# Expert places in alternating sizes, with gather, transposes and sums in blocks, in a two-layer diffusion backbone with a routed expert layer

## The chip, the cores and the metric

The kernel runs on one core of a Trainium2 chip. The metric is the device time of one execution in microseconds (us), here the median of three runs.

## The reference

Two layers work on 256 latent tokens behind 256 context tokens, width 1024, all in float32. The first layer is attention beside a convolution, then a dense SwiGLU. The second is a bidirectional state-space mixer, then a layer of eight experts, of which each token uses two. Only the expert layer is touched:

```python
D_MODEL, SEQ, N_EXPERTS, TOP_K, D_FF_EXPERT = 1024, 256, 8, 2, 3584
def swiglu(h, w1, w3, w2):
    return (silu(h @ w1) * (h @ w3)) @ w2
def moe_swiglu(h, w_router, w1, w3, w2):          # h: 256 tokens x 1024
    top_v, top_i = lax.top_k(h @ w_router, TOP_K)
    gates = sum(one_hot(top_i, 8) * softmax(top_v)[..., None], axis=1)
    for e in range(N_EXPERTS):
        out = out + gates[:, e:e+1] * swiglu(h, w1[e], w3[e], w2[e])
    return out
```

The weights of one expert are three matrices of 1024 x 3584 float32, 44.04 MB; eight make 352.3 MB, and each is read once. After this layer come the residual and a last RMS norm.

## The kernel before

All weights are streamed from DRAM. In the expert part a load fills one of 16 SBUF buffers of 1 MB, taken in turn (`ring`, L1637; `net.rings` in `build`), and SyncE's queue (SP) issues every load (L131). A load waits until TensorE (PE) has read what its buffer held before. So DMA can be at most 16 loads ahead of PE.

`run` (L150) goes through a list of units; a unit has views (the loads, called pieces here), a function per 128 weight rows and an end. It places the load of a later piece (`AHEAD` = 14 pieces further) ahead of the current piece's matmuls. The framework then orders each engine's instructions by priority in program order, as operands become ready.

**Places.** There are eight places for experts. Place 0 holds expert 0, whose weights have fixed addresses; places 1 to 7 hold the other experts by falling token count (`places`, L1579), and their loads use a register that SP reads. A place has room for 32 tokens in each of its groups: `G = [3, 3, 3, 3, 2, 2, 2, 2]`. If an expert has more tokens than its place, two conditional passes over all eight experts follow (`moe`, L1643).

**One expert** (`expert`, L1471). `gather` (L1432) compares each token's position with slot numbers (DVE, L1444), and 16 matmuls with that 0/1 matrix collect the tokens, transposed (PE, L1451), which ACT and DVE scale and write to SBUF (L1457, L1459). `up` multiplies by w1 and w3: the hidden width is cut into a part of 2048 (16 pieces of 1 MB: 8 KB per row) and one of 1536 (16 pieces of 768 KB: 6 KB per row). Each group's 32 tokens take 32 columns of the array, and four slices of the width are multiplied side by side, 8 instructions per piece and group in the trace (L1491). SiLU is on ACT (L1499), the product on DVE (L1502). `turn` transposes the hidden values (PE, L1514), and ACT and DVE copy them out (L1519, L1517). `down` multiplies by w2 (L1545), 14 pieces of 1 MB, each two blocks of 128 rows of 4 KB. `scatter` scales the result (DVE, L1555), multiplies with the transposed 0/1 matrix (PE, L1562; the transposes of that matrix are L1466) and adds the gated rows to the stream (DVE, L1566).

**Order.** `experts` (L1627) chains the units: the first `up` of an expert, then the second half of the `down` of the one before and its scatter, then the first transposes, the second `up`, the first half of `down`, the second transposes. Gather, transposes of the 0/1 matrix and scatter are generators that `tick` (L202) advances in the gaps between pieces, so their PE work stands between matmuls of other pieces. `finish` (L1669) does the last norm and stores the output.

Of the kernel before, what the change touches and what calls it, by code (L numbers as in the profile page):

```python
# [19 lines left out]
P = 128  # L20
# [7 lines left out]
NCONST = 1032  # L28


def host_consts():

    kc = np.zeros((P, NCONST), np.float32)
# [12 lines left out]
    ang = np.concatenate([row[:, None] * inv, col[:, None] * inv], axis=-1).astype(f32)  # L46
    cos, sin = np.cos(ang), np.sin(ang)
    cd = np.repeat(cos, 2, axis=1)
    sd = np.stack([-sin, sin], axis=-1).reshape(2 * P, 64)
    kc[:, C_COS:C_COS + P] = cd.reshape(2, P, 64).transpose(1, 0, 2).reshape(P, P)  # L50
    kc[:, C_SIN:C_SIN + P] = sd.reshape(2, P, 64).transpose(1, 0, 2).reshape(P, P)
    for j in range(4):
        kc[32 * j:32 * j + 8, C_SEL8:C_SEL8 + 8] = np.eye(8)
    return kc


class Pair:
# [4 lines left out]
    def __call__(self, k, s=slice(0, 512)):  # L62
        return tuple(t[k // 4][:, k % 4, s] for t in self.t)

# [11 lines left out]
class Net:  # L76
# [44 lines left out]
    def load(self, view, pool=None):  # L121

        pieces = view if isinstance(view, list) else [(slice(0, P), view)]
# [161 lines left out]
    def columns2(self):  # L285
        A, cols, row = self.A, self.cols_fn, self.row_fn
        kc = self.ecp.tile([P, NCONST - C_LE], F32, name="kc")
        self.nc.sync.dma_start(kc, A["kc"][:, C_LE:])
# [1084 lines left out]
    def route(self):  # L1373
# [4 lines left out]
        self.h2 = mp.tile([P, 2, D], F32, name="h2")  # L1378
        m8 = rt.tile([P, 2, 8], F32, name="m8")
# [49 lines left out]
    G = [3, 3, 3, 3, 2, 2, 2, 2]  # L1429
    SS = ((0, 512), (2048, 384))  # L1430

    def gather(self, e, pos, n_g):  # L1432
# [4 lines left out]
        Pm = self.wk([P, 2, 3, 4, 32], "pm", bufs=2)[:, :, :n_g]  # L1437
        x = self.wk([P, KD, 96], "xe", bufs=2)[:, :, :n]
        PT = self.wk([P, 3, 256], "PT", bufs=2)

        def work():
            slots = self.iota[:, :n].rearrange("p (g t) -> p g t", g=n_g).unsqueeze(2).to_broadcast([P, n_g, 4, 32])
            for b in range(2):
                nc.vector.tensor_scalar(Pm[:, b], slots, pos[:, b, e:e + 1], None, op0=ALU.is_equal)  # L1444
            yield
            for q in range(2):
                pt = self.ps("h")
                for i in range(4):
                    k = 4 * q + i
                    for b in range(2):  # L1450
                        nc.tensor.matmul(pt[:, i * n:(i + 1) * n].rearrange("p (g t) -> p g t", g=n_g),  # L1451
                                         self.h2[:, b, k * P:(k + 1) * P], Pm[:, b, :, 0], start=b == 0, stop=b == 1)
# [7 lines left out]
                yield  # L1460

        def turn():
            for g in range(n_g):
                pt = self.ps("h")
                for b in range(2):
                    nc.tensor.transpose(pt[:, b * P:(b + 1) * P], Pm[:, b, g].rearrange("p r t -> p (r t)"), self.ident)  # L1466
                nc.scalar.copy(PT[:, g], pt[:, 0:256])
                yield
        return x, PT, work(), turn()

    def expert(self, e, n_g, nxt=None):  # L1471


        nc, A = self.nc, self.A
        w1, w3, w2 = (self.weights(n, e) for n in ("od_ex_w1", "od_ex_w3", "od_ex_w2"))
        st = {}

        def up(s, i, w):
            c0, n = self.SS[s]

            def begin():
                if s == 0 and i == 0:
                    st["x"], st["PT"], work, st["turn"] = self.xe
                    for _ in work:
                        pass
                st[i] = [self.ps("h") for _ in range(n_g)]
# [17 lines left out]
            return Unit([w[:, k:k + 1, c0:c0 + 4 * n] for k in range(KD)], mm, begin, end, False)  # L1504

        def turn(s):
            nch = self.SS[s][1] // P

            def call():
                st["hT", s] = hT = self.wk([P, 4, 3, P], "hT", bufs=2)  # L1510
                for g in range(n_g):
                    pt = self.ps("h")
                    for c in range(nch):
                        nc.tensor.transpose(pt[:, c * P:(c + 1) * P], st["g"][g][:, c * P:(c + 1) * P], self.ident)  # L1514
                    o, i = hT[:, :nch, g], pt[:, :nch * P].rearrange("p (c t) -> p c t", c=nch)
# [4 lines left out]
                if s == 0:  # L1520
                    self.later(st["turn"], self.R_GA)
                elif nxt is not None:
                    self.xe = nxt()
                    self.later(self.xe[2], self.R_GA)
            return Unit(begin=call)

        def down(s):
            nch = self.SS[s][1] // P
# [5 lines left out]
            def mm(k, wv, _):  # L1534

                p, c = divmod(k, nch)
                st["w", k % 2] = wv, p, c
                if k % 2 == 0:
                    return
                for g in range(n_g):  # L1540
                    for half in range(2):
                        for j in range(2):
                            w, p, c = st["w", j]
                            r = 64 * half + 32 * j
                            nc.tensor.matmul(st["y"][g][r:r + 32], st["hT", s][:, c, g, 32 * p:32 * p + 32],  # L1545
                                             w[:, 512 * half:512 * half + 512], start=s == 0 and k == 1,
                                             stop=s == 1 and k == 4 * nch - 1, tile_position=(0, r))

            k0 = 16 * s
            return Unit([w2[:, k0 + r:k0 + r + 2] for r in range(0, 4 * nch, 2)], mm, begin, None, False)  # L1550

        def scatter():
            ys = self.wk([P, 3, 512], "ys", bufs=2)
            for g in range(n_g):
                nc.vector.tensor_mul(ys[:, g], st["y"][g], self.g2)  # L1555
            yield
            for b in range(2):
                pt = [self.ps("h") for _ in range(2)]
                for g in range(n_g):
                    for half in range(2):  # L1560
                        r = slice(64 * half, 64 * half + 64)
                        nc.tensor.matmul(pt[half], st["PT"][r, g, b * P:(b + 1) * P], ys[r, g], start=g == 0,  # L1562
# [4 lines left out]
                yield  # L1567

        first = [up(0, 0, w1), up(0, 1, w3)]
        second = [turn(0), up(1, 0, w1), up(1, 1, w3), down(0), turn(1)]  # L1570
        return first, second, [down(1), Unit(begin=lambda: self.later(scatter(), 1))]

    def weights(self, name, e):
        w = self.A[name][0]
        if e == 0:
            return w[0].rearrange("(k p) n -> p k n", p=P)
        return w[bass.ds(self.at[e], 1)].rearrange("o (k p) n -> p (o k) n", p=P)

    def places(self):  # L1579
# [15 lines left out]
        nc.vector.tensor_tensor(one, sq(rank, 1), sq(self.iota[:, 0:7], 2), op=ALU.is_equal)  # L1595

        def place(dst, src):
# [6 lines left out]
        ati = mp.tile([P, 7], I32, name="ati")  # L1604
        nc.vector.tensor_copy(ati, at)
        self.at = {e: nc.values_load(ati[0:1, e - 1:e], engines=[mybir.EngineType.SP], min_val=1, max_val=7)
                   for e in range(1, 8)}
# [6 lines left out]
        self.pos, self.gate = pos, gate  # L1614
        cap = mp.tile([P, 8], F32, name="cap")
        for e in range(8):
            nc.gpsimd.memset(cap[:, e:e + 1], 32.0 * self.G[e])
        nc.vector.tensor_copy(over[:, 0:1], cnt[:, 0:1])
        place(over[:, 1:8], cnt[:, 1:8])
        nc.vector.tensor_sub(over, over, cap)  # L1620
# [4 lines left out]
        self.cap = cap  # L1625

    def experts(self, gather, n_g):  # L1627

        units, last = [], []
        for e in range(8):  # L1630
            nxt = (lambda e=e: gather(e + 1)) if e < 7 else None
            a, b, c = self.expert(e, n_g[e], nxt)
            units += a + last + b
            last = c
        return units + last
# [5 lines left out]
    AHEAD = 14  # L1641

    def moe(self):  # L1643
        nc = self.nc
        self.xe = self.gather(0, self.pos, self.G[0])
        for _ in self.xe[2]:
            pass
        self.places()
        units = self.experts(lambda e: self.gather(e, self.pos, self.G[e]), self.G)
        self.run(units, self.AHEAD)  # L1650
        self.fn = self.wk([P, D], "t8")
        nc.sync.dma_start(self.fn, self.A["final_norm"].partition_broadcast(P))
        self.drain()
# [4 lines left out]
        for q in (0, 1):  # L1658
            with self.tc.If(n > 96 * q):
                self.rings = [self.rawp]  # L1660
                p2 = self.wk([P, 2, 8], "p2", bufs=1)
                nc.vector.tensor_tensor(p2, self.pos, self.cap.unsqueeze(1).to_broadcast([P, 2, 8]), op=ALU.subtract)
                nc.vector.tensor_scalar(p2, p2, -96.0 * q, None, op0=ALU.add)
                self.xe = self.gather(0, p2, 3)
                self.run(self.experts(lambda e: self.gather(e, p2, 3), [3] * 8))
                self.drain()
# [89 lines left out]
def build(tc, A, out, dbg=None):  # L1756
# [6 lines left out]
    with ExitStack() as ctx, tc.tile_pool(name="cp", bufs=1) as net.cp, \  # L1763
# [3 lines left out]
        with tc.tile_pool(name="t8p", bufs=9) as net.t8p, ExitStack() as early:  # L1767
# [11 lines left out]
            with psum("psm", h=5, y=3) as net.psp, tc.tile_pool(name="mp", bufs=1) as net.mp:  # L1779
# [3 lines left out]
                with tc.tile_pool(name="ep", bufs=1) as net.wp, tc.tile_pool(name="rawm", bufs=1) as rawm:  # L1783
# [16 lines left out]
```

## Time and profile before

| what | us |
|---|---|
| runs | 1996.44 (median), 1993.87, 1998.35 |
| the profiled execution, its own time | 1998.1 |
| its span, first to last instruction | 1996.3 |
| first expert matmul (L1491) after the span's start | 1088.6 |
| PE busy in the span | 1860.1 (93%) |

The profile is of one execution. Times within it are counted from the start of its span. Engines are PE (TensorE), DVE (VectorE), ACT (ScalarE), POOL (GpSimd) and SP (SyncE's DMA queue). A busy PE is busy by its records, whose ends are modelled.

### The profile page before, as it was taken

Reading aid. Unit: us, or ns where it says so; the run is one execution under the profiler, and the core shown is the slowest. Engines: PE = TensorE matmul, PEld = TensorE weight load, DVE = VectorE, ACT = ScalarE, POOL = GpSimd, SP = SyncE. Lnnn points to the kernel's source line nnn. Section 1 sums busy time; section 2 is a strip of 40 time slices with the busy share of each in tenths; the row PEclk is TensorE's granted clock in tenths of the full one; section 3 lists DMA queues with packets and bytes.
Section 4 is the critical chain, followed back from the end, with each engine's and each line's share of the span. In section 5 each row is a group of like instructions: output and inputs, shape, how many; then the busy total and the mean of one; then the engine's idle time right before and its main releaser. Section 6 shows DMA issues by size and latency. Waiting matters only on the chain.

```text
span 1996.3 us, 29959 instructions
## 1 busy us (share of the span) xinstructions
PE 1860.1 (93%) x12586; PEld 1057.2 (53%) x12586; DVE 734.5 (37%) x1079; ACT 519.0 (26%) x948; POOL 257.7 (13%) x239
## 2 busy tenths in 40 slices
PE   6999999999999989899898999999999999979795
PEld 3685366888888868666566343433434343313121
DVE  3496545333343458988975000101001011101011
ACT  3434443222223247466653000000000000000000
POOL 0154000000000024476650000000000000000000
PEclk8999989999999999999898999999999999999998
DMA  8544575323322332221338999898998999999996
GB/s 295 179 136 155 202 201 179 127 85 106 106 85 95 117 118 85 84 64 64 116 127 313 306 418 364 336 403 289 416 344 342 415 389 416 413 417 413 418 413 236
DMA packets 136429, 488.31 MB, mean 245 GB/s; under 512 B 10432, under 2 KB 15192, under 8 KB 119896
## 3 DMA queue, kind: packets, MB, share of 16 engines
q1 hardware_dynamic: 136280, 486.25, 65.0%
q8 instruction: 103, 1.69, 0.4%
q14 instruction: 46, 0.38, 0.1%
HBM read 485.14 MB, written 1.07 MB: 244 GB/s over the span
## 4 chain that ended last, share of the span: by engine, by line
PE 69%; DMA 14%; DVE 10%; ACT 2%; issue 2%; POOL 1%; SPq 0%; DVEq 0%; ACTq 0%; POOLq 0%
PE h L1491 20%; PE g L226 9%; PE g L227 9%; PE g L228 9%; DMA t<-in_od_ex_w_dram 9%; PE y L1545 8%; DVE cv L1055 5%; DMA raw<-in_od_ex_w_dram 4%; PE h L1562 2%; PE g L330 1%; PE h L1451 1%; PE o L758 1%; PE g L735 1%; DVE whl L147 1%; DMA raw<-in_ev_w_in_dram 1%
## 5 line engine op out<-in xcount | busy, mean ns | idle before, releaser
L1491 PE MATMUL h<-t,xe 128*32 128x384 f32 (+1 forms) x2880 | 288.4, 541 | 13.5 <-DMA t<-in_od_ex_w_dram 13.3
L227 PE MATMUL g<-t,whl 128*128 128x512 f32 (+1 forms) x608 | 237.7, 391 | 0.0
L228 PE MATMUL g<-t,whl 128*128 128x512 f32 (+1 forms) x608 | 236.1, 394 | 0.7 <-POOL whl L147 0.7
L226 PE MATMUL g<-t,whl 128*128 128x512 f32 (+1 forms) x608 | 233.3, 395 | 1.4 <-ACT opad L1033 0.7
L1491 PE MATMUL h<-raw,xe 128*32 128x512 f32 (+1 forms) x2240 | 223.3, 540 | 8.1 <-DMA raw<-in_od_ex_w_dram 8.1
L147 DVE TENSOR_TENSOR whl<-raw,whl 128x1024 fp32r<-128x1024 f32 x109 | 138.6, 1274 | 201.0 <-ACT whl L144 200.6
L144 ACT CAST whl<-raw 128x1024 fp32r<-128x1024 f32 x129 | 134.7, 1050 | 265.6 <-PE g L228 231.2
L1491 PEld LDWEIGHTS h<-t,xe 128*32 128x32 f32 x2880 | 92.0, 110 | 195.3 <-issue 167.9
L1502 DVE TENSOR_TENSOR g<-g,h 128x512 f32<-128x512 f32 (+1 forms) x40 | 24.8, 621 | 458.3 <-PE h L1491 365.4
L411 POOL TENSOR_SCALAR rsv<-sst 128x1 f32<-128x1 f32 (+1 forms) x15 | 5.5, 364 | 1353.6 <-DVE sst L404 1353.5
L227 PE MATMUL g<-whl,t 128*128 128x512 f32 (+1 forms) x432 | 169.3, 394 | 6.4 <-DVE whl L147 3.2
L228 PE MATMUL g<-whl,t 128*128 128x512 f32 (+1 forms) x432 | 166.8, 394 | 0.0
L226 PE MATMUL g<-whl,t 128*128 128x512 f32 (+1 forms) x432 | 162.4, 395 | 2.9 <-DVE t L624 1.4
L1491 PEld LDWEIGHTS h<-raw,xe 128*32 128x32 f32 x2240 | 73.7, 110 | 150.9 <-issue 134.7
L1545 PE MATMUL y<-t,hT 128*32 128x512 f32 x1288 | 144.9, 594 | 8.7 <-DMA t<-in_od_ex_w_dram 8.6
L226 PEld LDWEIGHTS g<-t,whl 128*128 128x128 f32 x608 | 116.0, 192 | 30.1 <-issue 2.3
L228 PEld LDWEIGHTS g<-t,whl 128*128 128x128 f32 x608 | 116.0, 191 | 25.3 <-issue 1.9
L227 PEld LDWEIGHTS g<-t,whl 128*128 128x128 f32 x608 | 116.4, 191 | 23.4 <-issue 0.9
L1519 ACT COPY hT<-h 128x512 f32<-128x512 f32 (+1 forms) x24 | 12.8, 533 | 418.1 <-PE h L1514 417.8
L1545 PE MATMUL y<-raw,hT 128*32 128x512 f32 x952 | 107.9, 594 | 8.8 <-DMA raw<-in_od_ex_w_dram 8.8
L1545 PEld LDWEIGHTS y<-t,hT 128*32 128x32 f32 x1288 | 43.0, 110 | 103.0 <-issue 77.8
L227 PEld LDWEIGHTS g<-whl,t 128*128 128x128 f32 x432 | 82.5, 191 | 27.0 <-DVE whl L147 4.7
(348 smaller groups left out, 2189.3 us busy)
## 6 DMA issues: line engine op xcount, KB each, us to landing
t<-in_od_ex_w_dram SPq DMA_DIRECT2D x135, 1024.0 KB, 12.9
raw<-in_od_ex_w_dram SPq DMA_DIRECT2D x105, 1024.0 KB, 13.9
t<-in_od_ex_w_dram SPq DMA_DIRECT2D x72, 768.0 KB, 9.3
raw<-in_od_ex_w_dram SPq DMA_DIRECT2D x56, 768.0 KB, 10.8
raw<-in_ev_ff_w_dram SPq DMA_DIRECT2D x32, 1024.0 KB, 5.2
raw<-in_ev_ada_w_dram SPq DMA_DIRECT2D x24, 1024.0 KB, 6.9
raw<-in_od_ada_w_dram SPq DMA_DIRECT2D x24, 1024.0 KB, 5.3
raw<-in_od_w_in_dram SPq DMA_DIRECT2D x20, 1024.0 KB, 5.2
```

Source lines behind the costliest of these rows:

```text
L144: self.nc.scalar.copy(hv, v[:, k0:k0 + m])
L147: eng.tensor_tensor(lv, v[:, k0:k0 + m], hv.bitcast(F32), op=ALU.subtract)
L226: mm(out, l[0], r[0], start=start, stop=False)
L227: mm(out, l[0], r[1], start=False, stop=False)
L228: mm(out, l[1], r[0], start=False, stop=stop)
L330: nc.tensor.matmul(st["p"][32 * j:32 * j + 32], self.cs[:, k, 6 - 2 * i:38 - 2 * i], wv, start=k < 4, stop=k >= 4, tile_position=(0, 32 * j))
L735: nc.tensor.matmul(sc[c][:, :nk], self.qT[s, r, b * P:(b + 1) * P], self.kT[s, :nk], start=True, stop=True, tile_position=(64 * c, 0))
L1055: nc.vector.scalar_tensor_tensor(v, pads[i + j][:, 0:ns, t:t + 256], self.cvw(t, c0 + i + j), v, op0=ALU.mult, op1=ALU.add)
L1491: nc.tensor.matmul(st[i][g][32 * p:32 * p + 32, :n], st["x"][:, k, 32 * g:32 * g + 32], wv[:, n * p:n * p + n], start=k == 0, stop=k == KD ...
L1502: nc.vector.tensor_mul(st["g"][g], st["g"][g], st[1][g][:, :n])
L1545: nc.tensor.matmul(st["y"][g][r:r + 32], st["hT", s][:, c, g, 32 * p:32 * p + 32], w[:, 512 * half:512 * half + 512], start=s == 0 and k == 1,
L1562: nc.tensor.matmul(pt[half], st["PT"][r, g, b * P:(b + 1) * P], ys[r, g], start=g == 0, stop=g == n_g - 1, tile_position=(64 * half, 0))
```

## The change

- The groups of the places are now 3, 2, 3, 2, 3, 2, 3, 1. `RANKS` says which rank by token count goes to which place: the largest three of experts 1 to 7 to places 2, 4 and 6, the next three to 1, 3 and 5, the smallest to 7.
- Gather, transposes and scatter are blocks: gather of the next expert stands behind the second `up`, both halves of `down` follow each other, and scatter stands behind the first `up` of the next expert. No generators are left here.
- The transposed 0/1 matrix is no longer made by PE: the positions are written once to DRAM (`pos_rows`, in expert 0, between its w1 and w3), each expert reads its row of 256 positions back to all 128 partitions, and DVE compares it with slot numbers (`slot_map`).
- w2 is loaded as pairs of neighbouring rows, 8 KB, in 12 of the 14 pieces; the hidden values are transposed with a stride of two to match.
- Constants for slots, ranks and capacities are loaded in `route` (`km`). SP reads an expert's register at that expert's first load, no longer all seven in `places`. 17 buffers are in the ring, `AHEAD` is 16.

The diff, cut to its core:

```diff
+GROUPS = (3, 2, 3, 2, 3, 2, 3, 1)
+RANKS = (3, 0, 4, 1, 5, 2, 6)
...
+        km = mp.tile([P, 18], F32, name="km")
+        nc.sync.dma_start(km, self.A["kc"][:, NCONST:])
+        self.slot, self.rank_at, self.cap = km[:, 0:3], km[:, 3:10], km[:, 10:18]
...
-    G = [3, 3, 3, 3, 2, 2, 2, 2]
...
-        Pm = self.wk([P, 2, 3, 4, 32], "pm", bufs=2)[:, :, :n_g]
+        Pm = self.wk([P, 2, 96], "pm", bufs=2)[:, :, :n]
...
+    def slot_map(self, e, n_g):
+        nc = self.nc
+        r = self.wk([P, 256], "prow", bufs=2)
+        nc.sync.dma_start(r.rearrange("p (b t) -> p b t", b=2), self.posd[:, e].partition_broadcast(P))
+        PT = self.wk([P, 3, 256], "PT", bufs=2)
+        for g in range(n_g):
+            nc.vector.tensor_scalar(PT[:, g], r, self.slot[:, g:g + 1], None, op0=ALU.is_equal)
+        return PT
+
+    def pos_rows(self, pos):
...
+        nc.tensor.transpose(pt[:16, 0:P], pos.rearrange("p b e -> p (b e)"), self.ident)
+        r = self.wk([16, P], "posr", bufs=1)
+        nc.scalar.copy(r, pt[:16, 0:P])
+        d = self.drp.tile([16, P], F32, name=self.nm("posd"))
+        nc.sync.dma_start(d, r)
...
         def turn(s):
...
-                    for c in range(nch):
-                        nc.tensor.transpose(pt[:, c * P:(c + 1) * P], st["g"][g][:, c * P:(c + 1) * P], self.ident)
+                    for c in range(n // P):
+                        t = st["g"][g][:, c // 2 * 256:c // 2 * 256 + min(256, n - c // 2 * 256)]
+                        if t.shape[-1] == 256:
+                            t = t.rearrange("p (i j) -> p j i", j=2)[:, c % 2]
+                        nc.tensor.transpose(pt[:, c * P:(c + 1) * P], t, self.ident)
...
         def down(s):
+            pair = lambda w: w.rearrange("o (i j) n -> i (o j) n", j=2)
...
+        def evict():
+            st["PT"] = self.slot_map(e, n_g)
+            st["ys"] = ys = self.wk([P, 3, 512], "ys", bufs=1)
             for g in range(n_g):
                 nc.vector.tensor_mul(ys[:, g], st["y"][g], self.g2)
...
+        return ([Unit(begin=take), up(0, 0, "od_ex_w1"), up(0, 1, "od_ex_w3")],
+                [turn(0), up(1, 0, "od_ex_w1"), up(1, 1, "od_ex_w3")], [turn(1), down(0), down(1)],
+                Unit(begin=scatter))
...
         for e in range(8):
...
+            a, b, c, d = self.expert(e, n_g[e])
+            units += a + scatter + b + gather(e + 1) + c
+            if e == 0 and now:
+                units.insert(2, Unit(begin=now))
+            scatter = [d]
...
-    AHEAD = 14
+    AHEAD = 16
...
-                    net.rings = ["t8"] * 9 + [net.rawp] * 3 + [net.hlp] * 3 + [rawm]
+                    net.rings = ["t8"] * 9 + [net.rawp] * 3 + [net.hlp] * 3 + [rawm] * 2
```

## Rows read from the trace of the kernel before

**Rows 1.** The page, part 2: GB/s moved, in 40 slices of the span.

```profile
GB/s 295 179 136 155 202 201 179 127 85 106 106 85 95 117 118 85 84 64 64 116 127 313 306 418 364 336 403 289 416 344 342 415 389 416 413 417 413 418 413 236
```

**Rows 2.** Busy time by stretch: PE, PEld, DVE, ACT, POOL; clock, DMA share, GB/s.

```profile
1049.00:1088.00 39.00, 31.36 (x164) 25.98 (x163) 23.21 (x73) 14.20 (x25) 2.10 (x12) 0.87 0.93 357
1150.00:1200.00 50.00, 50.00 (x513) 21.78 (x509) 3.73 (x8) 2.69 (x6) 0.00 (x0) 1.00 1.02 418
1437.00:1560.00 123.00, 123.00 (x1185) 46.66 (x1186) 11.74 (x21) 8.19 (x17) 0.00 (x0) 1.00 0.94 357
1088.00:1655.00 567.00, 567.00 (x5448) 217.98 (x5451) 55.20 (x99) 40.05 (x82) 0.00 (x0) 1.00 0.95 363
1655.00:1748.00 93.00, 88.26 (x802) 29.70 (x795) 10.62 (x20) 6.17 (x14) 0.00 (x0) 1.00 1.02 414
1748.00:1855.00 107.00, 91.92 (x802) 28.78 (x802) 9.32 (x16) 5.61 (x12) 0.00 (x0) 1.00 1.02 415
```

**Rows 3.** The chain that ended last, from 1088 us: start, us, what.

```profile
1088.66 41.34 PE h L1491 x384
1130.00 1.53 PE h L1514 x12
...
1190.07 41.34 PE h L1491 x384
...
1313.53 41.34 PE h L1491 x384
...
1560.42 27.61 PE h L1491 x256
```

**Rows 4.** Timeline of SP's queue, 960 to 1092 us: start, us, what.

```profile
1077.13 0.33 SPq L131 DMA_DIRECT2D raw<-in_od_ex_w_dram  x1
1091.44 0.33 SPq L131 DMA_DIRECT2D t<-in_od_ex_w_dram  x1
```

**Rows 5.** Groups by line, 1190 to 1313 us: busy us, mean ns, idle before.

```profile
L1491 PE MATMUL h<-t,xe 128*32 128x512 f32 (+1 forms) x432 | 42.4, 540 | 0.0
L1491 PE MATMUL h<-raw,xe 128*32 128x512 f32 (+1 forms) x336 | 33.0, 540 | 0.0
L1545 PE MATMUL y<-t,hT 128*32 128x512 f32 x168 | 18.4, 592 | 0.0
L1545 PE MATMUL y<-raw,hT 128*32 128x512 f32 x168 | 18.4, 592 | 0.0
L1562 PE MATMUL h<-ys,PT 64*128 64x512 f32 x24 | 6.7, 606 | 0.0
...
L1466 PE MATMUL h<-ka,pm 128*128 128x128 f32 x6 | 1.3, 300 | 0.0
```

**Rows 6.** Timeline of PE where DMA sets the pace: pieces of 6, 8, 4 KB rows.

```profile
1723.10 1.50 PE L1491 MATMUL h<-t,xe 128*32 128x384 f32 x16 [0.38 <-DMA t<-in_od_ex_w_dram]
1725.00 1.50 PE L1491 MATMUL h<-t,xe 128*32 128x384 f32 x16 [0.41 <-DMA t<-in_od_ex_w_dram]
...
1748.01 1.92 PE L1491 MATMUL h<-raw,xe 128*32 128x512 f32 x16 [0.65 <-DMA raw<-in_od_ex_w_dram]
...
1785.24 1.92 PE L1491 MATMUL h<-raw,xe 128*32 128x512 f32 x16 [0.59 <-DMA raw<-in_od_ex_w_dram]
...
1792.90 1.92 PE L1545 MATMUL y<-t,hT 128*32 128x512 f32 x16 [0.64 <-DMA t<-in_od_ex_w_dram]
...
1800.55 1.92 PE L1545 MATMUL y<-t,hT 128*32 128x512 f32 x16 [0.61 <-DMA t<-in_od_ex_w_dram]
...
1855.30 1.92 PE L1491 MATMUL h<-raw,xe 128*32 128x512 f32 x16 [0.65 <-DMA raw<-in_od_ex_w_dram]
```

**Rows 7.** DMA issues: count, KB each, median us from issue to landing.

```profile
t<-in_od_ex_w_dram SPq DMA_DIRECT2D x135, 1024.0 KB, 12.9
...
dtpar<-in_od_dt_bias_f_dram SPq DMA_DIRECT2D x1, 16.0 KB, 2.8
```

**Rows 8.** Timeline of all engines behind the last landing.

```profile
1973.98 1.92 PE L1545 MATMUL y<-raw,hT 128*32 128x512 f32 x16 [0.62 <-DMA raw<-in_od_ex_w_dram]
...
1975.12 0.69 DVE L1555 TENSOR_TENSOR ys<-y,g2r 128x512 f32<-128x512 f32 x1 [33.54 <-PE y L1545]
1975.86 3.70 PE L1562 MATMUL h<-ys,PT 64*128 64x512 f32 x16
```

More of the change, by code (lines that the diff above doesn't have):

```diff
@@ L1502, in end, with take @@
                         nc.vector.tensor_mul(st["g"][g], st["g"][g], st[1][g][:, :n])
-            return Unit([w[:, k:k + 1, c0:c0 + 4 * n] for k in range(KD)], mm, begin, end, False)
+            view = lambda k: self.weights(name, e, [P, 1, 4 * n], lambda w: w[:, k * P:(k + 1) * P, c0:c0 + 4 * n]
+                                          .rearrange("o p n -> p o n"))
+            return Unit([view(k) for k in range(KD)], mm, begin, end, False)
+        def take():
+            st["x"] = self.xe
         def turn(s):
-            nch = self.SS[s][1] // P
+            n = self.SS[s][1]
             def call():
@@ L1519, in call @@
                         nc.scalar.copy(o, i)
[L1520 to L1524, printed above, removed]
             return Unit(begin=call)
         def down(s):
-            nch = self.SS[s][1] // P
+            r0, n = 4 * self.SS[s][0] // 4, self.SS[s][1]
+            rows = lambda r, m: (lambda w: w[:, r:r + m])
+            pair = lambda w: w.rearrange("o (i j) n -> i (o j) n", j=2)
+            pieces = []
+            for p in range(4):
+                for c in range(n // 256):
+                    f = rows(r0 + n * p + 256 * c, 256)
+                    pieces.append((lambda w, f=f: pair(f(w)), [(p, 2 * c), (p, 2 * c + 1)]))
+            if n % 256:
+                for p in (0, 2):
+                    f = rows(r0 + n * p, 2 * n)
+                    pieces.append((lambda w, f=f: f(w).rearrange("o (s i) n -> i (o s) n", s=2)[n - P:n],
+                                   [(p, n // P - 1), (p + 1, n // P - 1)]))
             def begin():
@@ L1542, in mm, with scatter @@
                         for j in range(2):
-                            w, p, c = st["w", j]
+                            p, c = at[j]
                             r = 64 * half + 32 * j
                             nc.tensor.matmul(st["y"][g][r:r + 32], st["hT", s][:, c, g, 32 * p:32 * p + 32],
[L1546 to L1553, printed above, removed]
+                                             st["w", j][:, 512 * half:512 * half + 512], start=s == 0 and k == 1,
+                                             stop=s == 1 and k == 4 * n // P - 1, tile_position=(0, r))
+            return Unit([self.weights("od_ex_w2", e, [P, 2, D], f) for f, _ in pieces], mm, begin,
+                        evict if s else None, False)
+        def evict():
+            st["PT"] = self.slot_map(e, n_g)
+            st["ys"] = ys = self.wk([P, 3, 512], "ys", bufs=1)
             for g in range(n_g):
                 nc.vector.tensor_mul(ys[:, g], st["y"][g], self.g2)
-            yield
+        def scatter():
             for b in range(2):
@@ L1566, in scatter, with weights, get @@
                     nc.vector.scalar_tensor_tensor(x, pt[half], self.gate[:, b, e:e + 1], x, op0=ALU.mult, op1=ALU.add)
[L1567 to L1577, printed above, removed]
+        return ([Unit(begin=take), up(0, 0, "od_ex_w1"), up(0, 1, "od_ex_w3")],
+                [turn(0), up(1, 0, "od_ex_w1"), up(1, 1, "od_ex_w3")], [turn(1), down(0), down(1)],
+                Unit(begin=scatter))
+    def weights(self, name, e, shape, f):
+        def get():
+            if e and e not in self.at:
+                self.at[e] = self.nc.values_load(self.ati[0:1, e - 1:e], engines=[mybir.EngineType.SP], min_val=1,
+                                                 max_val=7)
+            return f(self.A[name][0][bass.ds(self.at[e], 1) if e else slice(0, 1)])
+        return View(shape, get)
     def places(self):
@@ L1613, in places @@
                 place(dst[:, b, 1:8], src[:, b, 1:8])
[L1614 to L1617, printed above, removed]
+        self.gate = gate
+        self.pos2 = pos
         nc.vector.tensor_copy(over[:, 0:1], cnt[:, 0:1])
         place(over[:, 1:8], cnt[:, 1:8])
-        nc.vector.tensor_sub(over, over, cap)
+        nc.vector.tensor_sub(over, over, self.cap)
         mx = small("mxc", 1)
@@ L1624, in places, with experts, gather, call @@
         nc.vector.tensor_copy(self.cnt, mx)
-        self.cap = cap
-    def experts(self, gather, n_g):
-        units, last = [], []
-        for e in range(8):
[L1631 to L1635, printed above, removed]
+    def experts(self, n_g, now=None):
+        units, scatter = [], []
+        def gather(e):
+            def call():
+                self.xe, work = self.gather(e, n_g[e])
+                work()
+            return [Unit(begin=call)] if e < 8 else []
+        for e in range(8):
+            a, b, c, d = self.expert(e, n_g[e])
[3 more added lines that the diff above has]
+            scatter = [d]
+        return units + scatter
     def ring(self):
```

89 lines of the change are left out of this document (42 added, 47 removed).

## The prediction

> **What bounds the kernel now.** I read the throughput line first [rows 1]: from slice 22 on, at about 1090 us, the experts' weights stream. Up to slice 33 the rate swings between 289 and 418 GB/s, and from there to the end it stands at 413 to 418, but for single slices. The table by stretch says why [rows 2]. From 1088 to 1655 us PE is busy all the time (567 of 567 us), at a granted clock of 1.00, and DMA moves 363 GB/s. From 1655 to 1855 PE is busy 180 of 200 us and DMA moves 414 to 415. So two limits follow each other: PE for the places with three groups, DMA for those with two. The reader should see that each limit leaves the other resource idle in its half.
>
> The chain [rows 3] gives the sizes. The first product starts at 1088.66; a place with three groups takes 1313.53 - 1190.07 = 123.5 us; the fifth expert, the first with two groups, starts at 1560.42. In the DMA half the same step comes at 1748.01 and 1855.30 [rows 6], 107.3 us apart, and there PE waits 0.4 to 0.65 us for DMA before each piece. SP's queue [rows 4] shows how DMA is held back: after the load at 1077.13 all 16 buffers are taken (I count three expert loads before 1049 us and 13 from there), and the next goes out at 1091.44, when PE has read the first piece.
>
> **The change, part by part.**
>
> *Order of the places.* 567 us at 363 instead of 414 GB/s are 567 x (1 - 363/414) = 69.8 us of streaming lost to a full ring [rows 2]. Alternating places remove this if PE, over a pair, needs less than DMA. PE: of a three-group expert, 42.4 + 33.0 + 18.4 + 18.4 + 6.7 + 1.3 = 120.2 us are products that go by the number of groups [rows 5]; the third of them is 40.1. The transposes of the 0/1 matrix (1.3 for three groups) go. That leaves 122.2 us for three groups, 123.5 - 40.1 - 0.9 = 82.5 for two, some 43 for one. That a third is right shows in the first product, 41.34 against 27.61 [rows 3]. DMA: pieces land 37.23/15 = 2.48 us apart for 8 KB rows, 1.90 for 6 KB rows, 7.65/3 = 2.55 for w2's 4 KB rows [rows 6]. Before that is 16 x 2.48 + 16 x 1.90 + 14 x 2.55 = 105.8 us for an expert, 1.5 less than the 107.3 seen, which I add. After, with 12 of w2's pieces at 2.48, 106.5 us. A pair is 204.7 us on PE and 213 on DMA: DMA sets the pace, and 4 us per expert are free on PE. Three-group places let DMA gain 15 us on PE, two-group places take back 24; the ring holds some 40 us, so it neither fills nor matters after the first expert.
>
> *What stays lost.* Expert 0 begins with a full ring. From 1088 to 1091.4 nothing goes out: 3.4 us. Its first product reads 16 buffers in 41.3 us, refilled by 16 loads of 1.90: 10.9 us. The rest of expert 0, 80.9 us, frees 30 buffers, refilled in 30 x 2.49 = 74.7: 6.2. Together 20.5 us. The 17th buffer takes one more load ahead of 1088: -2.5.
>
> *w2 in 8 KB rows.* 8 x 12 x 0.07 = -6.6 us. Bounds: nothing if the rows go out as 4 KB after all, to 8 us if the other two pieces gain as well.
>
> *Slot map by comparison.* PE's transposes are counted above. Added are eight reads of 128 KB in 512 B rows. No row has such a read in a full stream. From below 128 KB at 414 GB/s, 0.3 us; from above the 2.8 us in which 16 KB land alone [rows 7], most of that latency. The step from 8 to 4 KB rows costs 0.07 us for 128 packets more, so 256 packets cost some 0.14: I take 0.5 us, +4 together, and keep 2 to 22. The DVE comparisons take the place of larger ones, on an engine that is idle nine tenths of the time [rows 2]. By the Trainium skill (DMA: Bandwidth & Descriptors, "Measured") a transfer of 64 KB takes 0.95 us; an estimate from that, 1.9 us for each read, would make the sum 11 us longer; no run here shows it.
>
> *Waits that are added.* The read stands on SP behind the next expert's first 16 loads. DVE waits for it; behind it on DVE stand the scaling of the result and the next expert's gate products, and PE waits for both in scatter. But those 16 loads are what PE works on until scatter, and the read lands right behind the last, so I take 0 to 3 us, within the 4 that are free. The one store of the positions lets SP wait until PE has transposed them, between w1 and w3 of expert 0; loads behind it wait for buffers of that same moment: 0 to 2 us. The constants' load stands beside the load of g2's row, which already waits for its memory: 0, at worst a few us of a stream that idles from about 1084 anyway. SP's register reads move to each expert's first load, where up to 16 loads are under way: 0.
>
> *Gather, transposes, sums in blocks.* The same PE instructions in another order. What hid DVE's gate product before the second transposes was half of `down`; now it is the gather. Where nothing covers it, in expert 0, the transposes start right at the end of the product and take 1.53 us [rows 3]. So 0 to 2 us for each expert, within the 4 free; if that cover is gone, each us costs 7 to 8 us.
>
> *Tail.* Before, the last piece lands at 1973.98 and the span ends 22.3 us later. With one group instead of two, half of the 3.70 us of sums and one scaling of 0.69 go [rows 8], and the last comparison, some 1 us, comes: -1.5.
>
> Sum: -69.8 + 20.5 - 2.5 - 6.6 + 4 - 1.5 = -55.9. Against the profiled execution's own time, 1998.1, that is 1942.2; this execution was 1.7 us over the median shown (1996.44), so a median of 1940.5.
>
> **The rivals.**
>
> *PE becomes the bound.* If waits of the blocks come to more than 4 us per expert, the pairs go by PE. At 8 us the excess is 4 x 7 = 28 us: 1968.5. For it: scatter uses four PSUM tiles at once and stands between products that need three, of five; the strided transposes may be slower. Against: the covers above, and 1.53 us without any.
>
> *The stream gives no more beside a busy PE.* In the first half DMA moves 357 to 363 GB/s because its rate is capped while PE never pauses, not because buffers are late. Then alternating brings nothing, and -6.6 + 4 - 1.5 are left: 1992.3. Against it stands one row: from 1150 to 1200 us PE is busy 50.00 of 50 us, and DMA moves 418 GB/s [rows 2]. The Trainium skill (DMA: Bandwidth & Descriptors, "Where 436 GB/s comes from") has a rule of this kind: from HBM a core gets some 358 GB/s, which binds. By that rule the first half is at the limit and the change is worth nothing there; the trace disagrees, with 414 GB/s and more from 1655 to 1855 us.
>
> *Slower: the position read comes late.* If SP sends the read only when the product that it should run beside is done, it lands behind a queue of loads, and scatter, and PE with it, waits each time. A load's median from issue to landing is 12.9 us [rows 7], a full queue is 16 x 2.5 = 40. The point from which this decides is (55.9/7) + 4 = 12 us per expert; at 20 us it is 7 x 16 = 112 us: 2052. For it: SP issues in order, and DVE stands still behind the read. Against: the read depends on nothing that is late, the 40 us of the next product stand between it and its use.
>
> *The places don't hold the tokens.* Then a second pass of eight experts would follow, over 850 us. On the reference's drawn inputs the router gives the experts 81, 90, 60, 39, 16, 83, 91 and 52 tokens. Ranked, 91, 90 and 83 fit 96, then 60, 52 and 39 fit 64, 16 fits 32, and expert 0's 81 fit 96. So its chance is 0.
>
> **How the numbers follow.** The forecast: 0.76. PE the bound, with a gain left: 0.14. The capped stream: 0.02. The late read: 0.06, half of it strong enough to come out slower than before, plus 0.02 for other mishaps of order. Late reads that still leave a gain are faster too; the capped stream and part of the borderline make "same". A measurement of this kernel tells about 0.2% from no change. So faster 0.91, same 0.03, slower 0.06. The range: down to 1928, where the full rate of 418 GB/s instead of 414 holds (8 us less) and expert 0 loses 4 us less; up to 1964, where the reads cost near their upper bound or the blocks expose 7 us per expert. That leaves out the rest of the PE case, the late read and the cap, somewhat under 2 in 10.
>
> **What would show it.** Right: from expert 1 on the rate stands at 412 or more in every stretch, PE waits for DMA at the end of each two-group expert, starts of a pair are some 213 us apart, the last landing is at about 1919, the place with one group has PE less than half busy, w2's pieces land 2.48 us apart. Wrong: PE busy throughout with the rate below 400 after expert 1 (the blocks), idle time of PE ahead of the sums (L1562 before) that ends with DVE or the position read (late read), a rate near 360 with free buffers (the cap), or a second pass.

## The result, and the profile after

The changed kernel takes 1943.2 us (median of four runs, 1940.9 to 1944.9), the kernel before in the same comparison 1995.2. The ratio is 0.9737, with a 95% interval of 0.9719 to 0.9755: 52.5 us less, against 55.9 in the forecast. The profiled execution took 1942.3 us, its span is 1940.4 us.

Busy time by stretch of the changed kernel, about one expert to a stretch (two are left out), then the end (columns as in [rows 2]; from 1391 us on PE begins an expert up to 19 us behind the start of its stretch):

```profile
1085.00:1201.00 116.00, 116.00 (x1162) 46.47 (x1165) 11.90 (x37) 9.11 (x18) 0.00 (x0) 1.00 0.92 357
1201.00:1285.00 84.00, 84.00 (x810) 33.28 (x806) 10.23 (x22) 4.93 (x10) 0.00 (x0) 1.00 1.02 417
1285.00:1391.00 106.00, 106.00 (x1061) 42.65 (x1057) 11.06 (x22) 6.80 (x14) 0.00 (x0) 1.00 1.02 418
1391.00:1494.00 103.00, 101.08 (x938) 35.65 (x934) 12.70 (x24) 4.96 (x10) 0.00 (x0) 1.00 1.02 418
...
1604.00:1706.00 102.00, 97.63 (x898) 33.72 (x890) 11.79 (x21) 4.96 (x10) 0.00 (x0) 1.00 1.01 418
...
1811.00:1916.00 105.00, 80.29 (x575) 17.70 (x571) 6.14 (x9) 2.15 (x4) 0.00 (x0) 0.83 0.96 396
1916.00:1941.00 25.00, 5.04 (x16) 1.18 (x8) 7.93 (x13) 2.89 (x8) 1.48 (x4) 0.57 0.14 49
```

Where [rows 2] had 363 GB/s over 567 us, the stream now stands at 417 to 418 from the second expert on, until it runs out in the last stretch, and it does so beside a PE that is busy 106 of 106 us. Only expert 0 is left at 357. There 116 x (1 - 357/418) = 16.9 us of streaming are lost, where 69.8 were lost before.

The chain that ended last (answering to [rows 3]) alternates with the places:

```profile
1085.71 20.74 PE h L1515 x192
...
1201.18 27.47 PE h L1515 x256
...
1285.54 41.20 PE h L1515 x384
...
1345.75 18.05 DMA raw<-in_od_ex_w_dram
...
1706.54 23.38 PE h L1515 x216
```

The first product (L1515, L1491 before) starts at 1085.71. A two-group expert that does not wait takes 1285.54 - 1201.18 = 84.4 us (82.5 in the forecast). From 1345 us on DMA stands in the chain, which it did not before 1668 us in the old kernel. The whole stage, first product to last landing, is 1915.3 - 1085.7 = 829.6 us; before it was 1974.0 - 1088.7 = 885.3.

SP's queue of the changed kernel (answering to [rows 4]) shows the full ring and the reads that the change adds:

```profile
1074.28 0.81 SPq L148 DMA_DIRECT2D raw<-in_od_ex_w_dram  x2
1088.91 17.93 SPq L148 DMA_DIRECT2D t<-in_od_ex_w_dram  x8
1107.27 0.33 SPq L1498 DMA_DIRECT2D posd<-posr  x1
1111.12 1.43 SPq L1483 DMA_DIRECT2D prow<-posd  x2
...
1549.41 0.38 SPq L1483 DMA_DIRECT2D prow<-posd  x1
```

The last load of the full ring goes out at about 1075, the next at 1088.91. The position reads are not behind the loads that I put them behind: four of the eight go out by 1117 us, and the last at 1549, hundreds of us ahead of its use. The framework moves a read forward as soon as a buffer for it is free.

PE's timeline where DMA sets the pace (answering to [rows 6]; L1586 is the product with w2), and the last piece:

```profile
1696.50 1.92 PE L1586 MATMUL y<-t,hT 128*32 128x512 f32 x16 [0.57 <-DMA t<-in_od_ex_w_dram]
1698.99 1.92 PE L1586 MATMUL y<-t,hT 128*32 128x512 f32 x16 [0.56 <-DMA t<-in_od_ex_w_dram]
1701.52 1.92 PE L1586 MATMUL y<-t,hT 128*32 128x512 f32 x16 [0.61 <-DMA t<-in_od_ex_w_dram]
1704.05 1.92 PE L1586 MATMUL y<-t,hT 128*32 128x512 f32 x16 [0.61 <-DMA t<-in_od_ex_w_dram]
...
1915.33 1.93 PE L1586 MATMUL y<-raw,hT 128*32 128x512 f32 x8 [0.58 <-DMA raw<-in_od_ex_w_dram]
```

w2's pieces now land 2.49 us apart, the last two of an expert, which kept 4 KB rows, 2.53. The last piece lands at 1915.33 and the span ends 25.1 us later, where it was 22.3 before. Eight instructions take as long there (1.93 us) as sixteen did in [rows 8]: the granted clock is 0.83 in the last stretch of the stream and 0.57 in the end, with one group of work for each piece. These are means of times at PE's two levels, 1.2 and 2.4 GHz.

### The profile page after: what moved, and what is told of

It reads as the page before. It is cut to its first block, busy times and chain, and to the rows that moved or that the text cites. A ratio compares the mean times of both kernels' runs of the same rounds, so it can differ in the third digit from the quotient of the medians.

```text
span 1940.4 us, 29063 instructions
## 1 busy us (share of the span) xinstructions
PE 1810.1 (93%) x12164; PEld 1046.5 (54%) x12164; DVE 732.0 (38%) x1093; ACT 509.5 (26%) x927; POOL 257.3 (13%) x231
## 4 chain that ended last, share of the span: by engine, by line
PE 65%; DMA 17%; DVE 11%; ACT 3%; issue 2%; POOL 1%; SPq 0%; ACTq 0%; DVEq 0%; POOLq 0%
PE h L1515 19%; PE g L243 9%; PE g L244 9%; PE g L245 9%; DMA raw<-in_od_ex_w_dram 8%; DMA t<-in_od_ex_w_dram 8%; PE y L1586 6%; DVE cv L1072 6%; PE h L1605 1%; PE g L347 1%; PE h L1468 1%; PE o L775 1%; PE g L752 1%; DVE whl L164 1%; DMA raw<-in_ev_w_in_dram 1%
## 5 line engine op out<-in xcount | busy, mean ns | idle before, releaser
L1515 PE MATMUL h<-t,xe 128*32 128x512 f32 (+1 forms) x2576 | 254.4, 544 | 6.5 <-DMA t<-in_od_ex_w_dram 6.5
L1515 PE MATMUL h<-raw,xe 128*32 128x384 f32 (+1 forms) x2288 | 226.7, 542 | 8.3 <-DMA raw<-in_od_ex_w_dram 8.3
L1515 PEld LDWEIGHTS h<-t,xe 128*32 128x32 f32 x2576 | 89.8, 110 | 160.4 <-issue 122.4
L1515 PEld LDWEIGHTS h<-raw,xe 128*32 128x32 f32 x2288 | 80.8, 110 | 141.2 <-issue 104.7
L1586 PE MATMUL y<-t,hT 128*32 128x512 f32 x1168 | 135.8, 616 | 10.7 <-DMA t<-in_od_ex_w_dram 10.7
L1523 ACT ACTIVATE g<-h 128x512 f32<-128x512 f32 (+1 forms) x38 | 20.7, 544 | 442.9 <-PE h L1515 442.9
L245 PEld LDWEIGHTS g<-t,whl 128*128 128x128 f32 x608 | 115.9, 191 | 25.1 <-issue 1.9
L1586 PE MATMUL y<-raw,hT 128*32 128x512 f32 x960 | 111.1, 613 | 5.0 <-DMA raw<-in_od_ex_w_dram 5.0
L1597 DVE TENSOR_TENSOR ys<-y,g2r 128x512 f32<-128x512 f32 x19 | 13.1, 692 | 248.3 <-PE y L1586 248.3
```

The costliest lines, as they stand in the source:

```text
L245: mm(out, l[1], r[0], start=False, stop=stop)
L1515: nc.tensor.matmul(st[i][g][32 * p:32 * p + 32, :n], st["x"][:, k, 32 * g:32 * g + 32], wv[:, n * p:n * p + n], start=k == 0, stop=k == KD ...
L1523: nc.scalar.activation(st["g"][g], st[0][g][:, :n], AF.Silu)
```

## The experiments

Differences below are those of the ratios to the kernel before in the same comparison, against 0.9737 for the changed kernel, times 1995 us. The interval of a ratio is some 0.002 to either side, so such a difference is good to about 5 us. Where it helps, the length of the stage in the profiled execution is given too, first product to last landing (829.6 us in the changed kernel, 885.3 before): it leaves out the start and the end of the kernel.

**The order alone, taken away.**

```diff
-GROUPS = (3, 2, 3, 2, 3, 2, 3, 1)
-RANKS = (3, 0, 4, 1, 5, 2, 6)
+GROUPS = (3, 3, 3, 3, 2, 2, 2, 2)
+RANKS = (0, 1, 2, 3, 4, 5, 6)
```

> The changed kernel with the old order and sizes of the places (3, 3, 3, 3, 2, 2, 2, 2 groups, by falling count); all else as changed. Theory (the order keeps DMA streaming): while the four large places run, PE sets the pace and the ring is full, so most of the 70 us of lost streaming come back; carried load by load I get 45 us over the changed kernel, 1988 us (1980 to 1996), rate about 360 to 370 GB/s over the first four experts. Rival (the other parts made the gain: one group fewer, 8 KB rows, the 17th buffer, blocks): at most 10 us over the changed kernel, 1953 or less.

Measured: 1986.2 us, ratio 0.9939 (0.9918 to 0.9960), 40 us over the changed kernel; the stage is 874.8 us, 45 longer. Busy time by stretch, the four large places and the rest:

```profile
1090.00:1570.00 480.00, 480.00 (x4697) 188.06 (x4693) 47.86 (x101) 29.72 (x60) 0.00 (x0) 1.00 0.93 362
1570.00:1960.00 390.00, 348.68 (x3136) 114.76 (x3132) 37.88 (x68) 17.73 (x36) 0.00 (x0) 1.00 1.01 417
```

(This kernel has one group more, in a place where PE waits for DMA.) The two limits are back, one behind the other: 362 GB/s beside a PE without a pause, then 417 beside one that waits.

**The order alone, put into the kernel before.**

```diff
-    G = [3, 3, 3, 3, 2, 2, 2, 2]
+    G = [3, 2, 3, 2, 3, 2, 3, 1]
+    RANKS = [3, 0, 4, 1, 5, 2, 6]
...
-        nc.vector.tensor_tensor(one, sq(rank, 1), sq(self.iota[:, 0:7], 2), op=ALU.is_equal)
+        rank_at = mp.tile([P, 7], F32, name="rankat")
+        for i, r in enumerate(self.RANKS):
+            nc.gpsimd.memset(rank_at[:, i:i + 1], float(r))
+        nc.vector.tensor_tensor(one, sq(rank, 1), sq(rank_at, 2), op=ALU.is_equal)
```

> The kernel before with nothing changed but the sizes and order of its places (3, 2, 3, 2, 3, 2, 3, 1) and the ranks that go with them; generators, PE-made 0/1 transposes, 4 KB rows of w2, 16 buffers stay. Theory: nearly all the gain, less 8 KB rows (7 us) and one buffer (2.5 us), plus no position reads (4 us): 46 to 52 us below before, 1943 to 1950 us, rate 410 to 416 GB/s from the second expert on. Rival (the other parts made the gain): within 15 us of before.

Measured: 1949.4 us against 1997.6, ratio 0.9769 (0.9746 to 0.9792): 46 us less than before; the stage is 837.7 us, 48 shorter. Its stretches, expert 0 and most of the rest:

```profile
1088.00:1204.00 116.00, 116.00 (x1163) 43.89 (x1159) 7.49 (x14) 9.42 (x20) 0.00 (x0) 1.00 0.96 359
1204.00:1900.00 696.00, 679.12 (x6276) 246.64 (x6268) 72.38 (x124) 42.77 (x90) 0.00 (x0) 0.99 1.02 413
```

From both sides, the order is worth 40 to 46 of the 52 us, and 45 to 48 of the 55.7 by which the stage became shorter. All the rest of the rewrite is worth some 6 to 12.

**w2's rows.**

```diff
-                        t = st["g"][g][:, c // 2 * 256:c // 2 * 256 + min(256, n - c // 2 * 256)]
-                        if t.shape[-1] == 256:
-                            t = t.rearrange("p (i j) -> p j i", j=2)[:, c % 2]
+                        t = st["g"][g][:, c * P:(c + 1) * P]
...
-            pair = lambda w: w.rearrange("o (i j) n -> i (o j) n", j=2)
+            pair = lambda w: w.rearrange("o (j i) n -> i (o j) n", j=2)
```

> The changed kernel with w2 in two blocks of 128 rows of 4 KB for each piece, and transposes without a stride. Theory: 96 pieces land 0.07 us later each, 6.6 us over the changed kernel, w2's pieces 2.55 us apart where DMA sets the pace. Rival (row size costs nothing in a full stream, the 418 GB/s have another cause): no change within 2 us. Third: the strided transposes cost PE more than the rows give, then it is faster than the changed kernel.

Measured: 1951.5 us (1942.9 to 1956.4), ratio 0.9763 (0.9736 to 0.9790), 5 us over the changed kernel; the intervals overlap, so the time alone does not settle it. The trace does: its stage is 837.1 us, 7.5 longer, where 6.6 were foreseen. First two pieces of w2 in a row, then one stretch of this kernel:

```profile
1704.95 1.92 PE L1584 MATMUL y<-t,hT 128*32 128x512 f32 x16 [0.62 <-DMA t<-in_od_ex_w_dram]
1707.52 1.92 PE L1584 MATMUL y<-t,hT 128*32 128x512 f32 x16 [0.64 <-DMA t<-in_od_ex_w_dram]
```

```profile
1201.00:1900.00 699.00, 669.48 (x6284) 242.94 (x6276) 73.16 (x136) 37.46 (x76) 0.00 (x0) 0.98 1.02 414
```

and the same stretch of the changed kernel:

```profile
1201.00:1900.00 699.00, 673.61 (x6284) 247.87 (x6276) 71.92 (x135) 37.41 (x76) 0.00 (x0) 0.98 1.01 417
```

The pieces are 2.57 us apart instead of 2.49, and the rate falls to the 414 that the kernel before had. Its 414 GB/s were no limit of the stream: they were the mean over rows of 8, 6 and 4 KB.

**The small place second.** `GROUPS = (3, 1, 3, 2, 3, 2, 3, 2)`, `RANKS = (6, 0, 3, 1, 4, 2, 5)`.

> The changed kernel with the place of one group second instead of last: 3, 1, 3, 2, 3, 2, 3, 2. Theory (DMA sets the pace, where the small place stands does not matter): the last landing stays within 3 us; only the end changes, as PE keeps its higher clock with two groups: the time from last landing to the end falls from 25.1 to about 22.5 us; total 0 to 4 us below the changed kernel. Rival (the ring's lead is needed from place to place, and a small place early wastes it): 10 us or more over the changed kernel.

Measured: 1941.8 us, ratio 0.9719 (0.9702 to 0.9736), 4 us less by ratio, 1.4 by medians, not resolved. The last landing is at 1915.70, 0.4 us from that of the changed kernel: where the small place stands does not matter to the stream. The end took 24.6 us, not the 22.5 of the theory. Over the fourteen traces of this study the end lies between 21.4 and 25.1 us, and it falls into two parts at the last DVE instruction of the norm (L1728). Up to the end of that instruction two groups take 13.0 us, here and in the kernel before. One group takes 11.5 to 13.3 us, in the same order in which the eight instructions of the last product take 1.06 to 1.94 us. Here is first the changed kernel (13.3 us; its last product is shown above), then the run in which PE makes the 0/1 matrix (11.6 us; told below), from the last product on:

```profile
1918.07 3.78 PE L1605 MATMUL h<-ys,PT 64*128 64x512 f32 x8 [0.81 <-DVE ys L1597]
...
1927.88 0.75 DVE L1728 TENSOR_SCALAR t<-t,rs 128x1024 f32<-128x1024 f32 x1 [0.95 <-POOL rs L430]
```

```profile
1911.21 1.07 PE L1585 MATMUL y<-raw,hT 128*32 128x512 f32 x8 [1.47 <-DMA raw<-in_od_ex_w_dram]
1913.18 1.99 PE L1604 MATMUL h<-ys,PT 64*128 64x512 f32 x8 [0.91 <-DVE ys L1596]
...
1922.02 0.75 DVE L1727 TENSOR_SCALAR t<-t,rs 128x1024 f32<-128x1024 f32 x1 [0.95 <-POOL rs L430]
```

So one group saves 1.5 us of the end at the higher clock, and PE's lower level (1.2 GHz) takes that back. The second part, in which the last store of the output goes out, takes between 9.3 us (the kernel before) and 12.3 (the run with 4 KB rows), and what sets it stays open.

**The price of a position read, two tries.**

```diff
+        for _ in range(4):
+            r2 = self.wk([P, 256], "prow2", bufs=4)
+            nc.sync.dma_start(r2.rearrange("p (b t) -> p b t", b=2), self.posd[:, e].partition_broadcast(P))
```

> The changed kernel with each expert's read of its positions issued four more times, into buffers that nobody reads: 32 reads more, 128 KB in 512 B rows each. Theory (0.5 us of stream each, as I took): 16 us over the changed kernel (10 to 22). Rival 1 (the estimate from the page, 1.9 us each): 61 us. Rival 2 (a read costs the 2.8 us of the small load alone): 90 us. If the reads cost only their bytes, 0.3 us, 10 us.

Measured: 1973.7 us, ratio 0.9893, 31 us over the changed kernel, 0.97 us for each read, between the theory and Rival 1. But all 32 went out between 1113 and 1198 us, before expert 0 had ended, and they held up the other loads: SP sent nine loads of weights between 1113 and 1153 us, some 19 in the changed kernel. So the try was made again, each set of reads held back by a small DVE instruction that reads it:

```diff
+        self.more = [self.wk([P, 256], "prow2", bufs=4) for _ in range(4)]
+        for r2 in self.more:
+            nc.sync.dma_start(r2.rearrange("p (b t) -> p b t", b=2), self.posd[:, e].partition_broadcast(P))
...
+            for r2 in self.more:
+                j = self.wk([P, 1], "junk", bufs=2)
+                nc.vector.tensor_tensor(j, r2[:, 0:1], ys[:, 0, 0:1], op=ALU.mult)
```

> Again four more reads of the positions for each expert, but each set is read by a small DVE instruction behind the expert's scaling, so that the next set cannot go out earlier than that: the reads are spread over the stage. If a read costs 0.95 us of stream: 27 to 33 us over the changed kernel. If 0.5 us: 13 to 19. If the 30 us of the first try came from their crowding in expert 0 (SP's queue, landing order) and not from a price for each: under 10 us.

Measured: 1972.0 us, ratio 0.9887 (0.9872 to 0.9902), 30 us over the changed kernel, 0.94 us for each read (by the stage 29.2 us, 0.91). The stretch that stands at 417 GB/s in the changed kernel is now at 406, and shows the price spread over the stage:

```profile
1201.00:1900.00 699.00, 663.68 (x6177) 242.47 (x6169) 73.47 (x160) 36.88 (x75) 0.00 (x0) 0.99 1.00 406
```

128 KB at 418 GB/s would take 0.31 us, so two thirds of the price are not the bytes. Two things may make them: the 256 rows of 512 B, or that all 128 partitions read the same 1 KB of DRAM. No run here separates the two.

**More PE work in each expert.** The gather's matmuls done twice, and five times:

```diff
-                    for b in range(2):
+                    for b in list(range(2)) * 2:
```

> The changed kernel with the gather's matmuls of every expert done twice: some 3.7 us more on PE for each expert. Theory (DMA sets the pace, 3 to 4 us per expert are free on PE): 3 to 7 us over the changed kernel, 3.7 of which are expert 0's own gather ahead of the stage. Rival (PE is the bound after all): 8 x 3.7 = 30 us over it.

Measured: 1949.3 us, ratio 0.9763 (0.9744 to 0.9782), 5 us over the changed kernel, where 30 would be PE's. The stage is 1.7 us longer; the rest lies ahead of it, where expert 0's own gather stands.

> The same with the gather done five times: some 15 us more on PE for each expert. Theory: 15 us ahead of the stage for expert 0's own (some of it while the ring is full anyway), then PE becomes the bound, each expert after the first costs 15 less the 4 that are free: 6 to 7 x 11 = 66 to 77, together 80 to 92 us over the changed kernel. Rival (much more PE time is free than I counted): under 50 us. Rival (PE is the bound already): 8 x 15 = 120 us.

Measured: 2037.8 us, ratio 1.0215 (1.0189 to 1.0242), 95 us over the changed kernel, a little above the 80 to 92 of the theory; 80 of them lie in the stage. The chain of this kernel:

```profile
1229.01 27.47 PE h L1515 x256
...
1284.75 18.04 PE h L1468 x160
1327.66 41.20 PE h L1515 x384
...
1460.65 27.47 PE h L1515 x256
```

A pair takes 1460.65 - 1229.01 = 231.6 us here, all PE's, and DMA can do one in 2 x 44.04 MB / 418 GB/s = 211. The gather took 3.7 and takes 18.0: 14.3 us more in each expert, 28.6 in a pair, of which 231.6 - 211 = 21 come out as time. So 8 us of a pair were free, 4 in each expert, as counted. The two runs bracket the point at which PE takes over.

**The floor of the stream.** One group in every place.

```diff
-GROUPS = (3, 2, 3, 2, 3, 2, 3, 1)
+GROUPS = (1,) * 8
...
-    kc[:, C_CAP:C_CAP + 8] = 32 * np.array(GROUPS)
+    kc[:, C_CAP:C_CAP + 8] = 256
```

> The changed kernel with one group in every place: at most 32 tokens for each expert are computed, the others are left out, and no second pass follows. All weights are still streamed. Theory (the stream is the floor, and only expert 0 holds it back): the 17 us of streaming lost in expert 0 go and nothing else, 1922 to 1930 us, rate 418 GB/s throughout. Rival (a busy PE slows the stream a little): the rate goes above 421 GB/s and the time falls below 1918 us.

Measured: 1923.5 us, ratio 0.9642 (0.9619 to 0.9665), 19 us below the changed kernel.

```profile
1085.00:1130.00 45.00, 37.48 (x328) 12.97 (x328) 4.28 (x16) 5.85 (x12) 0.00 (x0) 0.93 0.94 377
1130.00:1900.00 770.00, 534.82 (x2961) 119.42 (x2959) 44.58 (x90) 24.19 (x52) 0.00 (x0) 0.71 1.01 415
```

With less than half of the PE work, the second stretch streams at 415 GB/s as a whole, its running out included, and at 418 to 419 from 1200 to 1800 us, hardly faster than beside a busy PE. All that PE still costs the changed kernel is some 19 us, 17.2 of them in the stage, about the 16.9 lost in expert 0.

**PE makes the transposed 0/1 matrix again, and the buffers of the ring.**

```diff
-        nc.sync.dma_start(r.rearrange("p (b t) -> p b t", b=2), self.posd[:, e].partition_broadcast(P))
...
+            for b in range(2):
+                nc.tensor.transpose(pt[:, b * P:(b + 1) * P], Pm[:, b, g].rearrange("p r t -> p (r t)"), self.ident)
+            nc.scalar.copy(PT[:, g], pt[:, 0:256])
```

> The changed kernel with the transposed 0/1 matrix made by PE again (as a block behind the last half of down), without the store of the positions, the eight reads and the wide comparisons. Theory (a read costs the stream what the four-fold reads showed, 30 us / 32 = 0.95 us, PE has 3 to 4 us free per expert and this takes 1.3 at most): 4 to 8 us below the changed kernel. Rival (0.5 us for each read, as I predicted): 2 to 4 us below. Rival (the PE-made matrix stands in PE's way at each expert's end): 5 us or more above.

Measured: 1935.1 us, ratio 0.9705 (0.9691 to 0.9718), 6 us (8 by medians) below the changed kernel. The two profiled spans are 7.0 us apart. Of these, 1.0 lies ahead of the first product, 2.9 in the end, with the difference in clock that is told above, and 3.2 in the stage. Only the last can be put down to the reads. It is 0.4 us for each of the eight, 0.6 if the 1.3 us of transposes in expert 0 [rows 5], where PE sets the pace, stand against it in full: by these two traces less than an added read costs. Half of the eight go out in expert 0, where the stream is held up anyway; that this is the reason is not shown. The one part of the change that takes work from PE and gives it to DMA was a loss, of some 3 us.

> The same, with the place of one group second instead of last and an 18th buffer in the ring (the transposed matrix has one buffer for it). Theory: the stream starts one load further ahead, -2.5 us, the end is 1 to 3 us shorter: 7 to 13 us below the changed kernel, 1930 to 1936 us, the fastest. Rival (buffers are not what holds the stream in expert 0): no better than the run with PE's matrix alone.

Measured: 1935.4 us, ratio 0.9706: no better than with PE's matrix alone, against my theory. Its last piece lands at 1908.77, 2.4 us ahead of that run's 1911.21, as 18 buffers promised, but its end took 24.1 us against 22.2: with two groups it takes 13.1 us up to the norm's last instruction, with one, at the higher clock, 11.6.

> The changed kernel with 16 buffers in the ring instead of 17. Theory (only expert 0 meets a full ring, one load less ahead): 2.5 us over the changed kernel, 1 to 4. Rival (17 buffers are needed from place to place): 8 us or more. Rival (the number of loads under way is limited elsewhere): 0.

Measured: 1941.7 us, ratio 0.9738 (0.9724 to 0.9751): no difference. Again the last landing (1917.24) is 1.9 us later than with 17 buffers and the end (22.6 us) 2.5 shorter. The stretches of this kernel, then of the changed one:

```profile
1085.00:1127.00 42.00, 42.00 (x386) 14.13 (x389) 4.92 (x24) 4.07 (x7) 0.00 (x0) 0.99 0.73 245
1127.00:1165.00 38.00, 38.00 (x445) 21.55 (x437) 5.12 (x12) 4.26 (x9) 0.00 (x0) 1.00 1.01 412
```

```profile
1085.00:1127.00 42.00, 42.00 (x389) 13.95 (x388) 4.93 (x23) 4.07 (x7) 0.00 (x0) 0.99 0.79 270
1127.00:1165.00 38.00, 38.00 (x445) 21.65 (x445) 5.12 (x12) 4.50 (x10) 0.00 (x0) 1.00 0.97 393
```

The 17th buffer moves 25 GB/s x 42 us = 1.05 MB ahead, and two thirds of it are given back in the next 38 us, where the ring is full once more: with 16 buffers DMA is not held back there.

## Why the prediction was right

*Two limits in a row, and alternating places remove the first.* Right, and shown from three sides: taken out (+40 us), put in alone (-46 us), and in the rates, 418 beside a busy PE. The stage became 55.7 us shorter; my sum without the end was 54.4.

*PE and DMA for a pair.* I had 204.7 us for PE and 213 for DMA. PE without waits takes 84.4 for two groups; pairs begin at 1201.18, 1404.05 and 1613.49, so they take 203 us while the ring still gives its lead, then 209. Five-fold gathers put the free time at 4 us for each expert, as forecast. Two of the signs that I gave did not come: the first two-group expert does not wait for DMA (84 of 84 us busy), as the ring's lead lasts that long, and PE is not less than half busy with the last expert but 61 of 86 us, from 1830 to 1916 us, at a granted clock of 0.80.

*What stays lost in expert 0.* I had 20.5 us; the stretch shows 16.9. The term that was too large is the rest of expert 0: it contains no scatter, which I had counted (6.7 us).

*w2 in 8 KB rows.* -6.6 us foreseen; the pieces are 0.06 to 0.08 us closer, the stream 417 instead of 414 GB/s, the stage 7.5 us shorter than without them, the time 5 us, unresolved.

*Slot map by comparison.* The price that I had wrong: I took 0.5 us for a read, 4 us together. A read that is added costs 0.91 to 0.94 in the spread try, but leaving out all eight makes the stage 3.2 us shorter, 0.4 to 0.6 for each with PE's transposes. So 4 us for the eight was near, and as a price for a read in a full stream 0.5 was too low by nearly half. My value came from the step between 8 and 4 KB rows, which is 0.07 us for 128 rows more, 0.55 ns each; if the rows make the price, the short ones cost (0.94 - 0.31) us / 256 = 2.5 ns each over their bytes. What the Trainium skill (DMA: Bandwidth & Descriptors, "Measured") states for 64 KB in a transfer that GpSimd issues, 0.95 us, would by the same estimate have given 1.9, twice what the spread try measured. The value lay inside the bounds of 0.3 and 2.8.

*Gather, transposes, sums in blocks.* I allowed up to 2 us for each expert. The first pair is PE's throughout (203 of 203 us busy) and takes 202.9 us, where 204.7 were foreseen without any waits, so the blocks expose nothing that shows. No run takes them alone.

*Late reads.* They did not come late, for another reason than the one I gave: they go out early.

*The 17th buffer.* -2.5 us foreseen; 1.9 in the last landing, nothing that the time resolves.

*The end.* -1.5 us foreseen; it was 2.8 longer. The saving is there at the higher clock (11.5 to 11.6 us up to the norm's last instruction, 13.05 in the kernel before); the changed kernel's end ran at the lower one and took 13.3. That is the part I left out. The other 2.5 us lie behind that instruction (11.8 us, 9.3 before), and no run shows why.

*The first product* began 2.95 us earlier, for a reason ahead of any touched instruction: the lead is there at 1066 us already, where the same DVE instruction starts at 1065.90, 1068.88 before. In the traces of this study the first load behind the full ring goes out between 1088.0 us (PE's matrix) and 1094.1 (old order), with the same work ahead of it. This and the longer end cancel; that 1940.5 stands as near to 1943.2 as it does is in part luck.

*The capped stream.* The rule of the Trainium skill (DMA: Bandwidth & Descriptors, "Where 436 GB/s comes from"), some 358 GB/s for a core from HBM, is not what happened: the stream ran at 417 to 418 GB/s over 700 us. That section gets its figure by halving a stack's 716 GB/s between two cores, and this kernel runs on one.

## What to carry to other kernels

Where one stretch is held by an engine and the next by DMA, mix their work before speeding up either: with a ring of some 40 us, experts that are too heavy for PE by 13 us and experts too light by 21 (118.5 and 84.4 us of PE against 105.4 of DMA) can follow each other, and the stream never stops. Afterwards DMA is the limit, so work that moves from a busy engine to the DMA queue, like these position reads, costs time even if the engine looks full. Count how much is free on the engine that is second: here 4 us for each expert, and more than that costs at once.

## What the runs showed of the hardware

- A read of 1 KB of DRAM to all 128 partitions, 128 KB in 512 B rows, takes 0.91 to 0.94 us of a full stream, three times its bytes' share; 1 MB takes 2.48 us in 8 KB rows and 2.55 in 4 KB rows.
- A PE that never pauses takes hardly anything from the stream: 418 GB/s beside 106 of 106 busy us, 418 to 419 with one group in every place.
- With one group in every place the granted clock of PE was 0.71 over 770 us and products took longer, at no cost, as DMA set the pace. Behind the last landing the lower clock does cost: 13.3 against 11.5 us up to the norm's last instruction.
